# An expert layer that gathers rows of expert_v (and, for 64 tokens, of expert_u) in place of dense products

## The chip, the core and the metric
The kernel runs on one core of a Trainium2 chip. Its engines work beside each other, each in its own order of instructions: PE (TensorE, matrix products), DVE (VectorE), ACT (ScalarE), POOL (GpSimd) and SP, which only issues transfers here. The metric is the device time of one execution in microseconds, as the median of several runs; lower is better.

## What is computed
Two blocks are applied to 256 tokens of width 2048, all in float32. The first has a token mixer and then an expert layer; the second has gated linear attention with forgetting attention, and a state space layer. The change lies in the expert layer. With h the normed and modulated tokens, it is, shortened:

```python
def peer(h, w_pq, sub_keys, expert_u, expert_v):
    q = (h @ w_pq).reshape(B, T, 8, 2, 128)                      # 8 heads, two half keys
    s = einsum('bthpd,hpnd->bthpn', q, sub_keys)                 # 128 scores for each half key
    s1, i1 = top_k(s[..., 0, :], 16);  s2, i2 = top_k(s[..., 1, :], 16)
    cand_s, cand_i = all 256 sums s1 + s2, and i1 * 128 + i2
    top_s, pos = top_k(cand_s, 16);    idx = cand_i[pos];   g = softmax(top_s)
    act = gelu(einsum('td,ted->te', h, expert_u[idx]))           # 128 experts for a token
    return einsum('te,ted->td', g * act, expert_v[idx])
x = x + g2 * peer(...)
```

expert_u and expert_v have 16,384 rows of 2048 float32 each, 128 MB a table. Each token uses 128 rows of each.

## The kernel before
**Order of the work.** The program is written as one stream of main work, and side work is written as generators that wait in lists (`bg`, `bg2`, `bg3` and so on). `pump` takes the next piece of each list; the main loops call it at a rate set by `rate[0]` (pieces for each two sub-steps). So the place of side work in every engine's order is fixed when the program is built. `flush` runs what is left. `page` gives one of the 8 KB-wide buffers that all stages share, and an instruction that writes a page waits until its last user is done.

**Split products.** PE multiplies in a fast format that keeps only the upper part of a float32. A float32 operand is therefore split in two: ACT copies it into the fast format (`whi`, line 117) and DVE subtracts that copy from it (`wlo`, line 118). A product is then three matmuls: high by high, high by low, low by high.

**Dense expert layer.** After the key projection (`h2_part` makes the high and low parts `h2h` and `h2l` of the tokens, 16 slices of 128 channels), `u_unit(n)`, n from 0 to 63, computes the activation of all 16,384 experts for all 256 tokens. One unit takes two blocks of 128 experts: two loads of 1 MB of `u_t` (expert_u laid out by channels) from SP, the split, and 96 matmuls of 128x256 (lines 1281, 1282, 1286). ACT applies gelu, and POOL stores the unit's activations to `scr_a` in memory (line 1289).

Beside the units, `choose` finds for each token the 128 experts and the gates. `scatter(half, G)` turns these into a dense matrix of gates for one half of the experts: DVE makes one-hot matrices, POOL multiplies them by three parts of the gate (line 1362 before the change), PE multiplies the pair in bf16 (line 1377) and ACT copies the result out.

`Half.run` is the second product. For each block of 128 experts of its half, 1 MB of expert_v is loaded in rows from SP, split, and multiplied by the gated activations, in four banks of 512 columns for two tiles of 128 tokens (lines 1419, 1420, 1422). The order is: 47 units, with the first `scatter`; half 0 (`v0.run`), with `s5_prep`, which makes power tables for the state space layer; the other units, with the second `scatter`; half 1 (`v1.run`), whose last banks are finished one by one by `x2_end` and turned by `x2_turn` for the next projection.

**What follows.** The projection `ab_w_in` of the second block (lines 180 to 189) runs with `s5_prep2` as side work, which makes the other tables of the state space layer: DVE products, and 256 small matmuls (line 542).

In the names of tiles, `mm` and `sm` are PSUM banks, `raw` is a loaded block of weights, `x1T` holds the tokens by channels.

## Time and profile before

| | us |
|---|---|
| median of 3 runs | 3764.72 (3762.97 to 3765.24) |
| the profiled execution, its own time | 3766.24 |
| its span, first to last instruction | 3764.5 |
| PE busy | 3589.0 (95%) |
| DVE busy | 2660.7 (71%) |
| ACT busy | 1786.7 (47%) |
| POOL busy | 786.9 (21%) |

The mean granted clock of PE is 0.985 of its full speed. The program moves 754.19 MB, 200 GB/s in the mean. Busy time is no bound by itself: the stages have different limits, so the table is to be read together with windows of the trace, one for each stage, and with the times at which a stage begins and ends.

### The profile page before, as it was taken

The page shows a single profiled execution, that of the slowest core. Times are in us where ns is not written, and L with a number is a line of the kernel's source. Part 1 is how long each engine was busy: PE and PEld are TensorE (multiplying, and loading weights), DVE is VectorE, ACT ScalarE, POOL GpSimd, SP SyncE. Part 2 cuts the span into 40 slices and gives each one's busy share as a digit, 9 for nine tenths or more (in the row PEclk, how much of TensorE's full clock was granted, in tenths as well). Part 3 has the DMA queues.
Part 4 walks back from the last instruction along what each step waited for, and adds up shares of the span by engine and source line. Part 5 has one row for each costly group of instructions (what it writes and reads, how often), then busy time and mean ns, then how long its engine had stood idle before and what let it go on. Part 6 is the DMA issues. An engine that isn't in the chain of part 4 may idle for free.

```text
span 3764.5 us, 64975 instructions
## 1 busy us (share of the span) xinstructions
PE 3589.0 (95%) x24610; PEld 3151.5 (84%) x24610; DVE 2660.7 (71%) x4569; ACT 1786.7 (47%) x3619; POOL 786.9 (21%) x779
## 2 busy tenths in 40 slices
PE   6999999999999999999999998999999999988998
PEld 3788878887779999999887888888879977887896
DVE  2456896777658588887887589866577666677765
ACT  4323535644455444555545455555454445523464
POOL 2202210100101013554020067200042022142200
PEclk8999999999999999999999999999999999999999
DMA  9554573377654555555667544666545535675454
GB/s 370 223 224 166 173 254 122 108 273 269 239 186 155 198 191 194 196 186 197 243 235 261 190 141 155 253 224 218 197 160 201 190 111 185 222 210 182 147 198 166
DMA packets 155242, 754.19 MB, mean 200 GB/s; under 512 B 40608, under 2 KB 40896, under 8 KB 76464
## 3 DMA queue, kind: packets, MB, share of 16 engines
q1 hardware_dynamic: 116224, 661.78, 49.9%
q0 software_dynamic: 29232, 84.07, 6.9%
q10 hardware_dynamic: 9472, 4.20, 0.4%
q8 instruction: 192, 3.15, 0.3%
q14 instruction: 122, 1.00, 0.1%
HBM read 716.65 MB, written 33.19 MB: 199 GB/s over the span
## 4 chain that ended last, share of the span: by engine, by line
PE 77%; DVE 9%; DMA 5%; issue 4%; POOL 3%; ACT 2%; DVEq 0%; ACTq 0%; POOLq 0%; SPq 0%
PE mm L189 15%; PE mm L180 7%; PE mm L183 7%; PE mm L181 7%; PE sm L1281 5%; PE sm L1282 5%; PE sm L1286 5%; PE mm L1422 3%; PE sm L1422 3%; PE mm L1419 3%; PE sm L1420 3%; PE mm L1420 3%; PE sm L1419 3%; DVE wlo L118 3%; POOL oh L1362 1%
## 5 line engine op out<-in xcount | busy, mean ns | idle before, releaser
L118 DVE TENSOR_TENSOR wlo<-raw,whi 128x512 fp32r<-128x512 f32 x2096 | 1567.3, 765 | 844.1 <-ACT whi L117 749.9
L117 ACT CAST whi<-raw 128x512 fp32r<-128x512 f32 x2096 | 1274.5, 621 | 1607.9 <-PE mm L181 319.8
L1281 PE MATMUL sm<-h2h,whi 128*128 128x256 f32 x2048 | 513.6, 284 | 1.0 <-ACT whi L117 1.0
L1282 PE MATMUL sm<-h2l,whi 128*128 128x256 f32 x2048 | 507.4, 281 | 0.0
L1281 PEld LDWEIGHTS sm<-h2h,whi 128*128 128x128 f32 x2048 | 388.4, 190 | 1.2 <-ACT whi L117 1.2
L1282 PEld LDWEIGHTS sm<-h2l,whi 128*128 128x128 f32 x2048 | 387.4, 189 | 0.0
L1286 PE MATMUL sm<-h2h,wlo 128*128 128x256 f32 x2048 | 326.7, 281 | 10.3 <-DVE wlo L118 10.3
L1362 POOL TENSOR_TENSOR oh<-e,gpart 128x512 bf16<-128x512 bf16 x192 | 282.0, 1493 | 134.9 <-DMA raw<-in_expert_v_dram 51.0
L1286 PEld LDWEIGHTS sm<-h2h,wlo 128*128 128x128 f32 x2048 | 278.4, 189 | 12.0 <-DVE wlo L118 11.5
L180 PE MATMUL mm<-whi,hTh 128*128 128x512 f32 x576 | 230.6, 401 | 1.3 <-ACT whi L117 1.0
L181 PE MATMUL mm<-whi,hTl 128*128 128x512 f32 x576 | 227.2, 394 | 0.0
L189 PE MATMUL mm<-hTh,whi 128*128 128x256 f32 x704 | 180.2, 291 | 5.4 <-ACT hTh L611 2.4
L189 PE MATMUL mm<-hTl,whi 128*128 128x256 f32 x704 | 177.5, 285 | 3.4 <-DVE hTl L613 3.4
L183 PE MATMUL mm<-wlo,hTh 128*128 128x512 f32 x576 | 172.7, 397 | 1.9 <-DVE wlo L118 1.7
L189 PEld LDWEIGHTS mm<-hTh,whi 128*128 128x128 f32 x704 | 133.4, 190 | 19.2 <-issue 8.3
L189 PEld LDWEIGHTS mm<-hTl,whi 128*128 128x128 f32 x704 | 134.1, 191 | 7.6 <-DVE hTl L613 4.8
L189 PE MATMUL mm<-cnh,whi 128*128 128x256 f32 x512 | 136.3, 298 | 2.9 <-ACT whi L117 2.9
L180 PEld LDWEIGHTS mm<-whi,hTh 128*128 128x128 f32 x576 | 108.7, 189 | 31.3 <-issue 3.4
L183 PEld LDWEIGHTS mm<-wlo,hTh 128*128 128x128 f32 x576 | 108.1, 189 | 29.0 <-DVE wlo L118 3.8
L189 PE MATMUL mm<-cnl,whi 128*128 128x256 f32 x512 | 130.2, 287 | 0.0
L181 PEld LDWEIGHTS mm<-whi,hTl 128*128 128x128 f32 x576 | 108.6, 189 | 23.4
L1289 POOL DMA_DIRECT2D scr_a<-ua x64 | 36.4, 569 | 428.8 <-ACT ua L1288 417.4
(1562 smaller groups left out, 7829.0 us busy)
## 6 DMA issues: line engine op xcount, KB each, us to landing
raw<-in_u_t_dram SPq DMA_DIRECT2D x128, 1024.0 KB, 4.9
raw<-in_expert_v_dram SPq DMA_DIRECT2D x124, 1024.0 KB, 4.8
raw<-in_w_in_dram SPq DMA_DIRECT2D x80, 1024.0 KB, 4.9
raw<-in_ab_w_in_dram SPq DMA_DIRECT2D x56, 1024.0 KB, 4.9
raw<-in_wmodA_dram SPq DMA_DIRECT2D x32, 1024.0 KB, 8.7
mraw<-in_wmodB_dram SPq DMA_DIRECT2D x32, 1024.0 KB, 8.9
raw<-in_c_w_in_dram SPq DMA_DIRECT2D x32, 1024.0 KB, 5.1
mrn<-in_wmodB_dram POOLq DMA_DIRECT2D x64, 256.0 KB, 4.2
```

Of the source, the lines that this page charges most:

```text
L117: nc.scalar.copy(out=hi, in_=src)
L118: last_split[0] = nc.vector.tensor_tensor(out=lo, in0=src, in1=hi.bitcast(F32), op=OP.subtract)
L180: nc.tensor.matmul(o, lhsT=xh, rhs=wh, start=(k == 0), stop=False)
L181: nc.tensor.matmul(o, lhsT=xl, rhs=wh, start=False, stop=False)
L183: nc.tensor.matmul(ps[i][:], lhsT=X(k, tt)[0], rhs=wl, start=False, stop=(k == K - 1))
L189: nc.tensor.matmul(o, lhsT=w[:, j * 128:(j + 1) * 128], rhs=x, start=start, stop=stop, skip_group_check=True)
L1281: nc.tensor.matmul(o, lhsT=uh, rhs=xh, start=(k == 0 and r == 0), stop=False, skip_group_check=True)
L1282: nc.tensor.matmul(o, lhsT=uh, rhs=xl, start=False, stop=False, skip_group_check=True)
L1286: nc.tensor.matmul(o, lhsT=w_, rhs=x_, start=False, stop=(k_ == 15 and r == 1), skip_group_check=True)
L1362: nc.gpsimd.tensor_tensor(out=oh1[i][:], in0=e1[:], in1=gpart[:, i, tb:tb + 8, None].to_broadcast([128, 8, 64]), op=OP.mult)
L1419: nc.tensor.matmul(self.ps[tt][b][:], lhsT=hl[tt][0], rhs=vh, start=first, stop=False)
L1420: nc.tensor.matmul(self.ps[tt][b][:], lhsT=hl[tt][1], rhs=vh, start=False, stop=False)
```

## The change
Expert_v is no longer multiplied densely. For each token, its 128 rows are gathered with an indirect DMA (128 rows of 8 KB, 1 MB, one row in each partition), and summed over partitions with the gated activations as weights. `rows_of(t)` gathers for two tokens that lie 32 apart; `add_rows` makes the sums with eight matmuls of 32x512 in float32, of which four lie side by side in the array; the weights stand in one column of a `strip` that is zero elsewhere, so that 32 steps fill 32 rows of a bank. `part` multiplies a finished bank by g2 and adds it to the tokens.

The 256 tokens are treated in two ways. For the first NS = 64, expert_u is gathered by rows, too: `near()` gathers 64 times 128 rows (two tokens, half of their experts each), DVE multiplies them by the token and sums, and after gelu the 32 steps on expert_v follow. All that is side work under the u units. For the other ND = 192 tokens, the u units still compute all experts densely, but with 32 unsplit float32 matmuls of 128x192 in a unit; ACT's queue stores the activations to `scr_a`. Then `rest()` runs 96 steps for these tokens: gather the rows of two tokens, pick their 2 x 128 activations out of `scr_a` with two more indirect DMAs of single floats (`pick`), form the weights, add the rows. Gathers run three steps ahead, picks four.

`scatter`, its one-hot matrices and the split of expert_u and expert_v go. `choose` is kept and gives expert numbers and places in `scr_a`. `s5_prep` and `s5_prep2` are both side work of `rest` now; what POOL did in them is done by DVE, and their transfers go from SP. In `h2_part` POOL adds the shift for all 16 slices, and ACT copies the sum, so that `x1T` holds the tokens in float32 for the unsplit product.

The diff, cut to its core:

```diff
 def s5_prep():
-        V, G = nc.vector, nc.gpsimd
+        V, G = nc.vector, nc.sync
...
-                    tt(w0, Rim[:, ps_, 0:m], pi, OP.mult, G)
+                    tt(w0, Rim[:, ps_, 0:m], pi, OP.mult)
...
     def h2_part(kk):
...
-        nc.scalar.activation(out=h_, in_=t, func=AF.Identity, bias=s2c[:, kk:kk + 1])
-        if kk % 3 < 2:
-            nc.vector.scalar_tensor_tensor(out=l_, in0=t, scalar=s2c[:, kk:kk + 1], in1=h_.bitcast(F32),
-                                           op0=OP.add, op1=OP.subtract)
-        else:
-            nc.gpsimd.tensor_scalar(out=t, in0=t, scalar1=s2c[:, kk:kk + 1], scalar2=None, op0=OP.add)
-            nc.gpsimd.tensor_tensor(out=l_, in0=t, in1=h_.bitcast(F32), op=OP.subtract)
+        nc.gpsimd.tensor_scalar(out=t, in0=t, scalar1=s2c[:, kk:kk + 1], scalar2=None, op0=OP.add)
+        nc.scalar.copy(out=h_, in_=t)
+        (nc.gpsimd if kk % 3 == 2 else nc.vector).tensor_tensor(out=l_, in0=t, in1=h_.bitcast(F32), op=OP.subtract)
...
-    scr_a = dr.tile([64, 128, 512], F32, name="scr_a")
-    def u_unit(n):
-        a = t2([128, 512], F32, "ua")
-        ps = smb()
-        late = []
-        for r in range(2):
-            for k, uh, ul in wstream(A["u_t"][2 * n + r], 16, 128, 16):
-                o = ps[:, r * 256:r * 256 + 256]
-                xh, xl = h2h[k // 8][:, k % 8, :], h2l[k // 8][:, k % 8, :]
-                nc.tensor.matmul(o, lhsT=uh, rhs=xh, start=(k == 0 and r == 0), stop=False, skip_group_check=True)
-                nc.tensor.matmul(o, lhsT=uh, rhs=xl, start=False, stop=False, skip_group_check=True)
-                late.append((k, ul, xh))
-                if k % 4 == 3:
-                    for k_, w_, x_ in late:
-                        nc.tensor.matmul(o, lhsT=w_, rhs=x_, start=False, stop=(k_ == 15 and r == 1), skip_group_check=True)
-                    late.clear()
-        nc.scalar.activation(out=a[:], in_=ps[:], func=AF.Gelu)
-        nc.gpsimd.dma_start(out=scr_a[n], in_=a[:])
+    NS = 64
+    ND = 256 - NS
+    scr_a = dr.tile([128, 128, ND], F32, name="scr_a")
+    def u_unit(n):
+        a = t2([128, 2, ND], F32, "ua")
+        ps = mmb()
+        for r in range(2):
+            raw = page("uraw", [128, 16, 128]) if r else stm.tile([128, 16, 128], F32, name="raw", tag="raw", bufs=2)
+            nc.sync.dma_start(out=raw[:], in_=A["u_t"][2 * n + r])
+            for k in range(16):
+                if k % 4 == 0:
+                    half_step[0] += rate[0] / 2
+                    pump(int(half_step[0]))
+                    half_step[0] -= int(half_step[0])
+                nc.tensor.matmul(ps[:, r * ND:r * ND + ND], lhsT=raw[:, k, :], rhs=x1T[k // 8][:, k % 8, NS:256],
+                                 start=(k == 0 and r == 0), stop=(k == 15 and r == 1), skip_group_check=True)
+        nc.scalar.activation(out=a[:], in_=ps[:, 0:2 * ND].rearrange("p (a b) -> p a b", a=2), func=AF.Gelu)
+        nc.scalar.dma_start(out=scr_a[2 * n:2 * n + 2].rearrange("r p t -> p r t"), in_=a[:])
...
-    def scatter(half, G):
...
-    class Half:
...
+    def gather(dst, src, idx):
+        nc.gpsimd.indirect_dma_start(out=dst, out_offset=None, in_=src,
+                                     in_offset=bass.IndirectOffsetOnAxis(ap=idx.bitcast(U32), axis=0))
...
+    def rows_of(t):
+        r_ = [page("vrow", [128, 2048]) for _ in range(2)]
+        for c in range(2):
+            gather(r_[c][:], A["expert_v"], slot_e[:, t + 32 * c:t + 32 * c + 1])
+        return r_
+    def add_rows(bank, i, strip, r_, ms=(0, 1)):
+        for m in ms:
+            for g in range(4):
+                c, b = g % 2, 2 * m + g // 2
+                nc.tensor.matmul(bank[m][g * 32:g * 32 + 32, :], lhsT=strip[:, c, 31 - i:63 - i],
+                                 rhs=r_[c][:, b * 512:b * 512 + 512], start=(i == 0), stop=(i == 31),
+                                 tile_position=(0, g * 32), skip_group_check=True)
...
+    def near():
+        h2d = page("h2d", [128, 2048])
+        a2r, s2r = mod_row(4, "a2r"), mod_row(3, "s2r")
+        nc.scalar.activation(out=h2d[0:64, :], in_=x1[0][0:NS, :], func=AF.Copy, scale=r2[0:NS, 0:1])
+        nc.gpsimd.tensor_tensor(out=h2d[0:64, :], in0=h2d[0:64, :], in1=a2r[0:64, :], op=OP.mult)
+        nc.gpsimd.tensor_tensor(out=h2d[0:64, :], in0=h2d[0:64, :], in1=s2r[0:64, :], op=OP.add)
+        nc.gpsimd.dma_start(out=h2d[64:128, :], in_=h2d[0:64, :])
+        nc.vector.tensor_tensor(out=pair, in0=ident[:, 0:64], in1=ident[:, 64:128], op=OP.add)
+        while not chosen:
+            yield
+        rows = []
+        def load(j):
+            rows.append(page("urow", [128, 2048]))
+            gather(rows[-1][:], A["expert_u"], near_e[:, j:j + 1])
+        for j in range(3):
+            load(j)
+        yield
+        yield
+        for j in range(64):
+            t = rows.pop(0)
+            for p in range(2):
+                cs = slice(p * 1024, p * 1024 + 1024)
+                nc.vector.tensor_tensor_reduce(out=t[:, cs], in0=t[:, cs], in1=h2d[:, cs], scale=1.0, scalar=0.0,
+                                               op0=OP.mult, op1=OP.add, accum_out=near_f[:, p, j:j + 1])
+            if j < 61:
+                load(j + 3)
+            yield
+        nc.vector.tensor_tensor(out=near_f[:, 0], in0=near_f[:, 0], in1=near_f[:, 1], op=OP.add)
+        wide = t2([128, 128], F32, "wide")
+        nc.vector.memset(wide[:], 0.0)
+        for i in range(2):
+            h_ = slice(i * 64, i * 64 + 64)
+            nc.scalar.activation(out=wide[h_, h_], in_=near_f[h_, 0], func=AF.Gelu)
+        nxt = rows_of(0)
+        ps = smb()
+        nc.tensor.matmul(ps[:, 0:64], lhsT=wide[:], rhs=pair, start=True, stop=True)
+        nc.vector.tensor_tensor(out=act, in0=ps[:, 0:64], in1=slot_g[:, 0:NS], op=OP.mult)
+        near_bank.extend(smb() for _ in range(2))
+        yield
+        yield
+        for i in range(32):
+            strip = strips[i % 3]
+            nc.vector.tensor_copy(out=strip[:, :, 31], in_=act[:, i:i + 33:32])
+            add_rows(near_bank, i, strip, nxt)
+            if i < 31:
+                nxt = rows_of(i + 1)
+            yield
+            yield
+    def rest(done):
+        places = scr_a[:].rearrange("a b (c o) -> (a b c) o", o=1)
+        todo = [NS + 64 * q + i for q in range(3) for i in range(32)]
+        def pick(k):
+            a = t2([128, 2], F32, "picked")
+            for c in range(2):
+                t = todo[k] + 32 * c - NS
+                gather(a[:, c:c + 1], places, slot_a[:, t:t + 1])
+            return a
+        rows = {k: rows_of(todo[k]) for k in range(3)}
+        acts = {k: pick(k) for k in range(4)}
+        last = []
+        for k, t in enumerate(todo):
+            i, q = k % 32, k // 32
+            if k == 1:
+                g2.append(mod_row(5, "g2"))
+            if k == 3:
+                for b in range(4):
+                    part(near_bank, 0, 0, b, nc.vector)
+            if i == 0:
+                bank = [mmb() for _ in range(2)]
+            pump(4)
+            if k + 3 < len(todo):
+                rows[k + 3] = rows_of(todo[k + 3])
+            if k + 4 < len(todo):
+                acts[k + 4] = pick(k + 4)
+            strip = strips[k % 3]
+            nc.vector.tensor_tensor(out=strip[:, :, 31], in0=acts.pop(k)[:], in1=slot_g[:, t:t + 33:32], op=OP.mult)
+            if k + 2 >= len(todo):
+                last.append((i, strip, rows.pop(k)))
+                continue
+            add_rows(bank, i, strip, rows.pop(k))
+            if i == 31:
+                for b in range(4):
+                    part(bank, (q + 1) // 2, (q + 1) % 2, b, nc.vector)
+                    if q == 0:
+                        done(0, b)
+        for m in range(2):
+            for l in last:
+                add_rows(bank, *l, ms=(m,))
+            for b in (2 * m, 2 * m + 1):
+                part(bank, 1, 1, b, nc.vector)
+                done(1, b)
-    bg2.append(choose())
-    bg.append(scatter(0, G0))
-    rate[0] = 0.36
-    for n in range(UFIRST - 1):
-        u_unit(n)
...
+    bg2 += [choose(0), choose(1)]
+    bg3.append(near())
+    rate[0] = 2
+    for n in range(64):
+        u_unit(n)
+        rate[0] = 0.55
+    flush()
+    bg += [s5_prep(), s5_prep2()]
...
-    v1.run(x2_end, x2_turn)
+    rest(x2_end)
...
-    bg.append(s5_prep2())
-    rate[0] = 1.1
+    rate[0] = 0
```

How the instructions stand on the engines, at three places. First PE, in a u unit. Before, beside the first `scatter` (`oh` are one-hot matrices):

```order
L1281 MATMUL sm<-h2h_10307,whi 128x256
L1282 MATMUL sm<-h2l_10309,whi 128x256
L1286 MATMUL sm<-h2h_10307,wlo 128x256 x4
L1377 LDWEIGHTS oh_14843
L1377 MATMUL sm<-oh_14847,oh_14843 128x64
```

And after, in the units that have the 64 tokens' sums beside them (`uraw` is the unit's second block, `vrow` the gathered rows):

```order
L1382 MATMUL sm<-vrow,strip 32x512 x8
L1283 MATMUL mm<-x1T_9501,raw 128x192 x8
L1283 MATMUL mm<-x1T_9502,raw 128x192 x8
L1283 MATMUL mm<-x1T_9501,uraw 128x192 x8
L1283 MATMUL mm<-x1T_9502,uraw 128x192 x4
L1382 MATMUL sm<-vrow,strip 32x512 x8
```

The three split matmuls have become one unsplit matmul, and the eight narrow matmuls of a step (line 1382) stand where the one-hot products stood. The first 38 units have none of these; 29 of the 32 steps stand in the others.

Second POOL. Before, between the last of `s5_prep` in half 0 and the second `scatter` (line 1362 is the product of one-hot and gate there):

```order
L318 TENSOR_TENSOR s5w<-Rre,s5par 128x512
L414 DMA scr_r<-Rre 128x2x1024
L414 DMA scr_r<-Rim 128x2x1024
L441 DMA scr_p<-s5pw 128x640
L443 DMA scr_p<-s5par 128x64 x2
L1362 TENSOR_TENSOR oh_22976<-e_22974,gpart 128x512
L1362 TENSOR_TENSOR oh_22977<-e_22974,gpart 128x512
```

And after, from the middle of the u phase into `rest` (line 1362 is the indirect DMA of `gather` here):

```order
L1362 DMA urow<-in_expert_u_dram,near_e 128x2048 x54
L1362 DMA vrow<-in_expert_v_dram,slot_e 128x2048 x70
L1362 DMA picked<-scr_a,slot_a 128x1 x8
L1362 DMA vrow<-in_expert_v_dram,slot_e 128x2048 x2
L1362 DMA picked<-scr_a,slot_a 128x1 x2
L731 DMA g_15199<-scr_m_1407 128x2048
L1362 DMA vrow<-in_expert_v_dram,slot_e 128x2048 x2
```

POOL has no products left there: its row is gathers alone, 54 of expert_u, then 70 of expert_v (64 for the near tokens and 6 for the first three steps of `rest`), then two of rows and two of activations for each step. Each gather waits for the eighth software DMA before it.

Third PE, where the state space tables are made. Before, in the projection after the expert layer:

```order
L181 MATMUL mm<-whi,abl_29452 128x512
L180 MATMUL mm<-whi,abh_29450 128x512
L181 MATMUL mm<-whi,abl_29452 128x512
L183 MATMUL mm<-wlo,abh_29450 128x512 x2
L213 MATMUL sm<-ident,r_r 128x128 x2
L542 MATMUL sm<-s5c,s5bd 32x64 x8
L189 MATMUL mm<-abh_29449,whi 128x256
```

And after, in `rest`:

```order
L1382 MATMUL sm<-vrow,strip 32x512 x24
L1382 MATMUL mm<-vrow,strip 32x512 x112
L207 MATMUL sm<-ident,s5z 64x128 x8
L1382 MATMUL mm<-vrow,strip 32x512 x16
L542 MATMUL sm<-s5c,s5bd 32x64 x8
L1382 MATMUL mm<-vrow,strip 32x512
L542 MATMUL sm<-s5c,s5bd 32x64 x8
L1382 MATMUL mm<-vrow,strip 32x512 x7
```

The small matmuls of line 542 have moved from among the split matmuls of the projection to among the sums of gathered rows.

## Rows read from the trace of the kernel before

**Rows 1.** The page's shares: engine, busy us (share of the span), instructions.
```profile
PE 3589.0 (95%) x24610; PEld 3151.5 (84%) x24610; DVE 2660.7 (71%) x4569; ACT 1786.7 (47%) x3619; POOL 786.9 (21%) x779
```

**Rows 2.** Windows, expert layer: us, busy per engine, PEclk, DMA share, GB/s.
```profile
1231.00:1805.00 574.00, 565.76 (x5305) 562.59 (x5303) 448.05 (x696) 295.09 (x693) 199.42 (x152) 0.99 0.56 195
1805.00:2147.00 342.00, 338.99 (x1530) 280.59 (x1529) 263.95 (x530) 172.75 (x290) 40.63 (x43) 1.00 0.66 235
2147.00:2386.00 239.00, 220.34 (x2311) 213.15 (x2310) 203.40 (x188) 120.24 (x408) 142.97 (x105) 1.00 0.45 159
2386.00:2756.00 370.00, 361.89 (x1636) 300.10 (x1635) 240.52 (x349) 186.98 (x315) 20.74 (x17) 0.99 0.62 219
2756.00:2960.00 204.00, 195.24 (x1528) 178.43 (x1527) 158.04 (x385) 98.10 (x185) 57.51 (x55) 0.99 0.56 188
```

**Rows 3.** Timeline of PE at both ends: start us, us, engine, line, operation.
```profile
1231.13 0.36 PE L1281 MATMUL sm<-h2h,whi 128*128 128x256 f32 x1
2756.13 0.40 PE L180 MATMUL mm<-whi,abh 128*128 128x512 f32 x1
```

**Rows 4.** Timeline of POOL: two stores of activations, one for each u unit.
```profile
1290.49 0.54 POOL L1289 DMA_DIRECT2D scr_a<-ua  x1 [10.78 <-ACT ua L1288]
1301.81 0.54 POOL L1289 DMA_DIRECT2D scr_a<-ua  x1 [10.78 <-ACT ua L1288]
```

**Rows 5.** Timeline of PE: float32 matmuls of 256 and 129 columns, and one ahead.
```profile
633.76 0.64 PE L189 MATMUL mm<-hTh,wlo 128*128 128x256 f32 x4
634.24 1.89 PE L1053 MATMUL sm<-qT,kT 128*128 128x256 f32 x8
669.55 3.39 PE L1073 MATMUL sm<-vm,P 128*128 128x129 f32 x28 [0.98 <-DVE P L1064]
```

**Rows 6.** Groups of DVE by form: instruction, count | busy, mean ns | idle.
```profile
L682 DVE SCALAR_TENSOR_TENSOR macc<-mraw,sil,macc 128x2048 f32<-128x2048 f32 x30 | 70.4, 2345 | 2.1 <-DMA mraw<-in_wmodB_dram 2.1
```

**Rows 7.** Timeline of PE in the first stage: four narrow matmuls side by side.
```profile
53.86 1.94 PE L578 MATMUL sm<-raw,silz 128*32 128x512 f32 x8
100.09 1.06 PE L578 MATMUL sm<-raw,silz 128*32 128x512 f32 x8
101.09 0.62 PE L189 MATMUL mm<-hTh,wlo 128*128 128x256 f32 x3
```

**Rows 8.** Windows in the first stage, columns as in rows 2.
```profile
20.00:60.00 40.00, 25.05 (x134) 13.83 (x132) 9.93 (x32) 19.08 (x44) 2.56 (x4) 0.74 1.01 421
55.00:60.00 5.00, 4.30 (x29) 2.30 (x25) 0.94 (x6) 3.02 (x6) 0.64 (x2) 0.88 1.01 398
```

**Rows 9.** The page's DMA queues: packets, MB, share of 16 engines over the span.
```profile
q1 hardware_dynamic: 116224, 661.78, 49.9%
q10 hardware_dynamic: 9472, 4.20, 0.4%
```

**Rows 10.** DMA issues: engine, count, KB each, median us from issue to landing.
```profile
raw<-in_u_t_dram SPq DMA_DIRECT2D x128, 1024.0 KB, 4.9
scr_a<-ua POOLq DMA_DIRECT2D x64, 256.0 KB, 3.1
raw<-in_w_in_dram POOLq DMA_DIRECT2D x8, 1024.0 KB, 9.0
```

**Rows 11.** Groups of POOL by form, columns as in rows 6.
```profile
L1289 POOL DMA_DIRECT2D scr_a<-ua x64 | 36.4, 569 | 428.8 <-ACT ua L1288 417.4 <-DVE wlo L118 11.3
L1809 POOL DMA_DIRECT2D Tm<-scr_k x16 | 21.2, 1333 | 6.7 <-DVE vt L1797 5.5 <-PE sm L1913 1.2
L1362 POOL TENSOR_TENSOR oh<-e,gpart 128x512 bf16<-128x512 bf16 x192 | 282.0, 1493 | 134.9 <-DMA raw<-in_expert_v_dram 51.0 <-DVE e L1358 35.9 <-PE sm L1282 18.5
```

**Rows 12.** Groups of PE by form, line 542, columns as in rows 6.
```profile
L542 PE MATMUL sm<-s5c,s5bd 128*32 128x64 f32 x256 | 17.3, 220 | 0.0
```

**Rows 13.** Groups of POOL by form: the shift and the low part.
```profile
L1217 POOL TENSOR_SCALAR x1T<-x1T,s2c 128x256 f32<-128x256 f32 x5 | 8.0, 1608 | 99.9 <-ACT h2h L1212 99.9
L1218 POOL TENSOR_TENSOR h2l<-x1T,h2h 128x256 fp32r<-128x256 f32 x5 | 4.5, 897 | 0.4
```

286 lines of the change are left out of this document (94 added, 192 removed).

## The prediction

> **What bounds the kernel now.** I read the shares first: TensorE is busy 3589.0 of 3764.5 us [rows 1], so nearly every stage is its own. Then I cut the expert layer into stretches [rows 2]. It runs from the first matmul on expert_u, at 1231.13, to the first matmul of the next projection, at 2756.13 [rows 3]: 1525.0 us, in which PE is idle for 574 - 565.76 = 8 us, 3, 19 and 8 us in the four stretches, 38 us in all. Meanwhile the core moves only 159 to 235 GB/s. So this layer is bound by the number of columns that PE streams, and memory has room. In an undisturbed stretch one u unit (two blocks of 128 experts) takes 1301.81 - 1290.49 = 11.32 us [rows 4], which is 96 matmuls of 0.118 us. In the first 574 us 47 units are done, 12.2 us each, since the gate scatter shares PE.
>
> The change trades PE work for memory work, so the reader should price each of the two new phases twice, once by PE and once by bytes, and take the larger.
>
> **u phase: unsplit float32 for 192 tokens, all 64 units.** A unit has now 32 matmuls of 128x192. A float32 matmul shows as two records in the trace. Eight records of 256 columns take from 634.40 (633.76 + 0.64, the end before) to 636.13, 0.216 us each; 28 records of 129 columns end 3.39 us after their start, or (3.39 - 0.16)/28 = 0.115 us each, where 0.16 is the pipeline's fill (0.28 shown for a matmul that is spaced 0.12) [rows 5]. Between them 192 columns give 0.165 us by a straight line, 0.162 in proportion to columns. A unit has 64 records: 10.4 to 10.6 us. That is only 7% less than 11.32: the column count falls from 96 x 256 = 24,576 to 64 x 192 = 12,288, but a float32 record takes twice as long for a column. Sixty-four units: 664 to 700 us (the upper end allows 0.171 for a load of weights that isn't hidden); I take 680. ACT and DVE no longer split u, so they can't be late here.
>
> **64 near tokens, under the u phase.** u by rows is 64 gathers of 1 MB and 128 multiply-and-sum instructions of 128x1024 on DVE. The nearest row is a DVE instruction on 128x2048 float32 at 2345 ns [rows 6], so a gather's pair should cost 2.3 us, with 2 to 5 us as bounds, against some 30 units x 10.6 / 64 = 5.0 us that a gather has: hidden. v by rows is 32 steps of 8 narrow matmuls of 32x512, four side by side in the array. The same form runs in the first stage: 8 records (4 matmuls) take 1.0 us (100.09 to 101.09), and 1.94 at half clock [rows 7]. A step is 2.0 us; the order puts 29 steps into the u phase: +58. The one-hots go, POOL's 282.0 us [rows 11] and the matmuls that they feed; what PE lost to them lies inside the 1525.
>
> Now bytes. In the first stage the engines are full for 40 us and move 421 GB/s, 398 in the slowest 5 us [rows 8]; at 421 a transfer of 1024 KB (1 MB here, 1.049e6 bytes) takes 2.49 us. In units 7 to 37 lie 64 gathers, 61 loads of u and 6 MB of stored activations: 131 x 2.49 = 326 us beside 30 x 10.55 = 317 of PE. In the rest of the phase it is 70 gathers, 54 loads and 5 MB, 321 us beside 26 x 10.55 + 58 = 332. So both stand nearly level, and I add 10 us of stalls (0 to 40). u phase: 680 + 58 + 10 = **748** (722 to 798).
>
> **rest: v by rows for 192 tokens.** 96 steps of two 1 MB gathers, 6 of the 192 already issued: 186 x 2.49 = 463 us. Each step has also two gathers of 128 single floats. No row has packets of 4 bytes. The nearest are the 9472 small ones of q10, 4.20 MB in 0.4% of 16 engines' span [rows 9]: 0.004 x 16 x 3764.5 us / 9472 = 25 ns each. 256 packets over 16 engines would be 0.4 us a step, 38 us in all; 0 and 80 are my bounds, 40 my value. The state space tables, g2 and final_w add some 12 MB, 30 us. Two transitions (the first picks wait for the last stored activations, which take 3.1 us to land [rows 10], and the two last steps are held for the end) 15. rest: **548** (500 to 610). PE needs 2.0 to 4 us for a step of 5.7, so it is idle half the time and no bound even at half clock. DVE has the tables' work, which before cost at most all its 263.95 and 158.04 busy us of two stretches that were full of other work [rows 2]; it fits in 548.
>
> After rest come the last sums and the turn into the next projection, before hidden under banks of matmuls: +10 (5 to 15).
>
> **POOL's queue.** Every gather is issued from POOL, four to a step, and the order shows them in a row on POOL: vrow x2, picked x2. A direct DMA costs POOL 569 ns, one in 512 pieces 1333 [rows 11]. Four issues are 2.3 to 5.3 us a step against 5.7 for the bytes: just hidden, and if not it decides (second rival). Each issue also waits for the eighth DMA before it on that queue, which keeps four row gathers in flight: 4 x 2.49 us, and direct loads of that size land in 4.9 us [rows 10].
>
> **Tables moved.** s5_prep2 leaves the stage of the next projection. There it had 256 matmuls on line 542, 17.3 us [rows 12], and part of PE's 204 - 195.24 = 8.8 idle us [rows 2]. I take -15 (bounds -10 and -26). Its DMAs now go on SP, on which nothing waits in rest; the matmuls stand among the gathers' sums, where PE has room.
>
> **h2_part.** POOL now adds the shift for all 16 slices ahead of ACT's copy, 16 x 1.61 + 5 x 0.90 = 30.2 us [rows 13], where the first block of the key projection has 16 x 12 x 0.118 = 22.7 us of PE: +6 (0 to 12).
>
> **Sum**, against the profiled execution: 748 + 548 + 10 - 1525 = -219; -15 + 6: -228. 3766.2 - 228 = 3538. That execution lies 1.5 us over the median of the runs, so **3537** is the forecast.
>
> **Rivals.**
> *1. The gathers don't reach the stream's rate.* The bytes of the two phases are 281e6 and 209e6 (stored activations and tables with them). The direct loads of the whole run, q1, moved 661.78 MB in 49.9% of 16 engines' span [rows 9], 661.78e6 / (0.499 x 3764.5 us) = 352 GB/s while they ran. At that rate the phases take 798 and 594 us; with 10 and 55 of stalls and picks 808 + 649 + 10 = 1467, and 3766.2 - 58 - 9 = 3699. For it: no row shows a row gather, and 1 MB on POOL's queue took 9.0 us to land where SP's took 4.9 [rows 10]. Against it: q1 has small packets too (5.7 KB in the mean), a gathered row is 8 KB, as in the direct load of expert_v, and 40 us at 421 are no peak of a moment. Level with before at 490e6 / (1525 + 9 - 75 us) = 336 GB/s.
>
> The Trainium skill, "DMA: Bandwidth & Descriptors", Specifications, gives about 358 GB/s as a core's limit from HBM; by that figure the sum would be an estimated 3676. The 421 of [rows 8] stand above it, so the trace doesn't agree, and the sum goes by the rows.
>
> *2. Slower: POOL's issue is the bound.* In rest POOL works through 380 issues one after another. If an indirect one costs T, rest is 380 x T as soon as that is over 548, from T = 1.44 us. Level with before at rest = 548 + 228 = 776, T = 2.04. At 2.5 us rest is 950 and the time 3940. For it: issue time on POOL grows with pieces, 569 ns to 1333 [rows 11], and an indirect DMA has 128 addresses to read. Against it: 512 pieces cost but 1.33, and 64 issues stand at 569 ns beside a DVE that was busy 448 of 574 us [rows 2]. The Trainium skill, "SBUF — State Buffer", the "DVE blocks DMA" trap, says that some DVE modes lock POOL out while it writes descriptors; these 569 ns don't show that.
>
> *3. The u phase waits.* PE and memory are level there; if the pages that gathers, h2d and u share come free late, each of 64 units may lose 1 to 3 us: 3600 to 3730.
>
> *4. Nothing in it.* If unsplit float32 were no faster than 11.32 a unit and both phases ran as rival 1, little were left: 64 x 11.3 + 58 + 10 + 649 + 10 = 1450, and with rival 3's waits on top 3730 to 3790.
>
> **Chances.** Forecast, 3465 to 3610: 0.60. Rivals 1 and 3, 3610 to 3740: 0.18. Rival 4: 0.04, half of it within 0.2% of before. Rival 2 and what else ends slower: 0.15. Below 3465: 0.03. The range 3465 to 3740 holds 0.78, close to eight in ten. 0.2% (7.5 us) is about what a measurement of this kernel can tell from no change: faster by more 0.82, within 0.02, slower 0.16.
>
> **What would show it.** Right: a u unit of 10.4 to 10.6 us in units 0 to 6, 12.5 after unit 38; the share of DMA near 1.0 and 390 to 425 GB/s from unit 7 to the end of rest; a step of rest 5.3 to 6.2 us; POOL waiting for DMAs, not issuing; the next projection's 204 us shortened by 10 to 26. Wrong: windows of rest at 300 GB/s with POOL's issues back to back (rival 2), or with POOL waiting and DMA share under 0.9 (rival 1); PE waiting for u loads (rival 3); float32 records of 192 columns over 0.175 us.

## The result, and the profile after

| | us |
|---|---|
| forecast | 3537 (3465 to 3740) |
| after, median of 4 runs | 3659.99 (3658.43 to 3669.56) |
| before, median of 4 runs beside them | 3763.84 (3758.38 to 3765.24) |
| ratio, 95% interval | 0.9733 (0.9721 to 0.9745) |
| profiled execution of after: own time, span | 3658.43, 3656.7 |

The kernel became 104 us faster. The sign and the range held; the size was less than half of the 227 forecast.

The two ends of the expert layer, and of its phases, stand in PE's timeline (start us, us, engine, line, operation; in brackets the idle time before, and what ended it):

```profile
2038.38 5.36 PE L1382 MATMUL sm<-vrow,strip 128*32 128x512 f32 x48
2053.52 6.90 PE L1382 MATMUL mm<-vrow,strip 128*32 128x512 f32 x48 [9.78 <-issue]
...
2660.56 1.92 PE L1382 MATMUL mm<-vrow,strip 128*32 128x512 f32 x12 [0.45 <-DMA vrow<-in_expert_v_dram,slot_e]
...
2664.33 0.73 PE L180 MATMUL mm<-whi,abh 128*128 128x512 f32 x2 [0.24 <-ACT abh L248]
```

The first unit starts at 1239.56 (1231.13 in [rows 3]). The u phase ends with the last narrow sums of `near`, at 2038.38 + 5.36 = 2043.7; `rest` ends at 2662.5; the next projection begins at 2664.33. Against the forecast's terms:

| term | forecast | measured |
|---|---|---|
| before the first unit (`h2_part`) | +6 | +8.4 |
| u phase | 748 | 804 |
| of it 64 units | 680 | 64 x 10.40 = 666 |
| of it 29 steps of sums | 58 | 29 x 2.07 = 60 |
| what is left: stalls, and the last 3 steps of sums | 10 | 78 |
| `rest` | 548 | 619 |
| from there to the next projection | 10 | 2 |
| behind it, 3656.7 - 2664.3 against 3764.5 - 2756.1 | -15 | -16 |

The miss of 120 us is thus 56 in the u phase and 63 in `rest` and its tail; everything else came out within 3 us. Of the 78, PE is idle for 54. Another 5.4 are the last three steps of sums (line 1 above), which the forecast's sum left out. Windows of PE alone in the u phase (us, busy, mean granted clock, DMA share, GB/s) show where:

```profile
1400.00:1500.00 100.00, 87.95 (x514) 0.95 1.02 424
1500.00:1600.00 100.00, 75.76 (x429) 0.88 1.00 414
1600.00:1700.00 100.00, 90.25 (x548) 0.95 0.77 281
1700.00:1800.00 100.00, 100.00 (x644) 1.00 0.91 347
1800.00:1900.00 100.00, 100.00 (x648) 1.00 0.96 368
```

From 1400 to 1600 the DMA engines are full, and PE is idle for 36 of 200 us; from 1600 the engines have room again. From 1700 to 2000 PE never stops. What PE waits for in the whole phase is u:

```profile
PE mm L1283 <- DMA raw<-in_u_t_dram: 49.3, 9, 13.5
```

And the windows of `rest`:

```profile
2040.00:2100.00 60.00, 26.27 (x132) 0.72 0.71 276
2100.00:2200.00 100.00, 48.50 (x280) 0.78 0.75 291
2200.00:2300.00 100.00, 65.96 (x412) 0.88 0.94 354
2300.00:2450.00 150.00, 108.69 (x414) 0.90 0.97 372
2450.00:2600.00 150.00, 109.21 (x415) 0.91 0.97 366
```

The forecast took 421 GB/s from [rows 8]. The first 230 us of `rest`, where the state space tables stand, run far under it, and the settled part, which is only rows, picks and sums, still 12% under. The operations that no row of before showed are now in the groups (line, engine, operation, count | busy us, mean ns | idle before):

```profile
L1362 POOL DMA_INDIRECT vrow<-in_expert_v_dram,slot_e x256 | 252.8, 988 | 502.5 <-PE mm L1283 175.0
L1420 DVE CUSTOM_DVE_ANT_0 urow<-urow,h2d 128x1024 f32<-128x1024 f32 x128 | 156.2, 1255 | 115.0 <-DMA urow<-in_expert_u_dram,near_e 85.0
L1362 POOL DMA_INDIRECT picked<-scr_a,slot_a x192 | 186.8, 973 | 108.3 <-issue 58.8
```

An indirect issue costs POOL 0.97 to 0.99 us in the mean, whether it brings 1 MB or 512 bytes, inside the 0.57 to 1.33 of [rows 11]; back to back they stand 1.25 us apart. Four of them are 5.0 us a step. The second rival, which decides from 1.44, is out. The DVE pair takes 2.5 us (2.3 forecast) and is hidden.

### The profile page after: what moved, and what is told of

It reads as the page before. It is cut to its first block, busy times and chain, and to the rows that moved or that the text cites. A ratio compares the mean times of both kernels' runs of the same rounds, so it can differ in the third digit from the quotient of the medians.

```text
span 3656.7 us, 51912 instructions
## 1 busy us (share of the span) xinstructions
PE 3237.9 (89%) x20002; PEld 2593.6 (71%) x20002; DVE 1845.5 (50%) x3741; ACT 1062.0 (29%) x2012; POOL 899.5 (25%) x959
## 5 line engine op out<-in xcount | busy, mean ns | idle before, releaser
L118 DVE TENSOR_TENSOR wlo<-raw,whi 128x512 fp32r<-128x512 f32 x1088 | 766.2, 720 | 539.1 <-ACT whi L117 458.1
L117 ACT CAST whi<-raw 128x512 fp32r<-128x512 f32 x1088 | 660.1, 620 | 941.7 <-PE mm L181 347.6
L1382 PE MATMUL mm<-vrow,strip 128*32 128x512 f32 x1536 | 383.2, 695 | 184.1 <-issue 90.5
L1283 PE MATMUL mm<-x1T,raw 128*128 128x192 f32 x2048 | 358.9, 334 | 49.3 <-DMA raw<-in_u_t_dram 49.3
L1283 PEld LDWEIGHTS mm<-x1T,raw 128*128 128x128 f32 x2048 | 345.5, 196 | 60.9 <-issue 60.9
L1362 POOL DMA_INDIRECT vrow<-in_expert_v_dram,slot_e x256 | 252.8, 988 | 502.5 <-PE mm L1283 175.0
L1283 PE MATMUL mm<-x1T,uraw 128*128 128x192 f32 x2048 | 350.3, 328 | 0.6 <-DMA uraw<-in_u_t_dram 0.6
L1283 PEld LDWEIGHTS mm<-x1T,uraw 128*128 128x128 f32 x2048 | 336.2, 191 | 16.0 <-issue 13.4
L1420 DVE CUSTOM_DVE_ANT_0 urow<-urow,h2d 128x1024 f32<-128x1024 f32 x128 | 156.2, 1255 | 115.0 <-DMA urow<-in_expert_u_dram,near_e 85.0
L1362 POOL DMA_INDIRECT picked<-scr_a,slot_a x192 | 186.8, 973 | 108.3 <-issue 58.8
```

Of the source, the lines that this page charges most:

```text
L117: nc.scalar.copy(out=hi, in_=src)
L118: last_split[0] = nc.vector.tensor_tensor(out=lo, in0=src, in1=hi.bitcast(F32), op=OP.subtract)
L1283: nc.tensor.matmul(ps[:, r * ND:r * ND + ND], lhsT=raw[:, k, :], rhs=x1T[k // 8][:, k % 8, NS:256], start=(k == 0 and r == 0), stop=(k == ...
L1362: nc.gpsimd.indirect_dma_start(out=dst, out_offset=None, in_=src, in_offset=bass.IndirectOffsetOnAxis(ap=idx.bitcast(U32), axis=0))
L1382: nc.tensor.matmul(bank[m][g * 32:g * 32 + 32, :], lhsT=strip[:, c, 31 - i:63 - i], rhs=r_[c][:, b * 512:b * 512 + 512], start=(i == 0), s ...
L1420: nc.vector.tensor_tensor_reduce(out=t[:, cs], in0=t[:, cs], in1=h2d[:, cs], scale=1.0, scalar=0.0, op0=OP.mult, op1=OP.add, accum_out=nea ...
```

## The experiments: rest

All kernels but the last two were run once; the four runs of the changed kernel lie up to 11 us apart.

**Rows without picks; rows in order; two queues.** Why is `rest` slower than the stream? The first three kernels each take away one thing: the picks, the scatter of the rows over memory (blocks of expert_v that lie together, from POOL), and the single queue (one of two rows by a direct load from SP).

```diff
 def pick(k):
-    gather(a[:, c:c + 1], places, slot_a[:, t:t + 1])   # twice
+    return near_f[:, 2, 0:2]              # e1: constant activations
 def rows_of(t):                           # e2: blocks, from POOL
-    gather(r_[c][:], A["expert_v"], slot_e[:, ...])
+    nc.gpsimd.dma_start(out=r_[c][:], in_=A["expert_v"][b0:b0 + 128, :])
+    # e3: for c == 1 alone, from nc.sync
```

> Leaves out the 192 gathers of single activations in rest: the weights are made from a constant in their place. In the changed kernel a settled step of rest (two row gathers) takes 5.71 us, 370 GB/s, where 421 GB/s would give 4.98. Theory A (POOL's feed): a gather holds POOL for 1.25 us (0.95 and 0.30 behind it), so four a step are 5.0 us, and with the waits for lanes and pages no queue of rows stands ready for the DMA engines. With two gathers a step POOL needs 2.5 us; the step falls to 5.0 to 5.1 us and the total by about 60 us, to 3600. Theory B (rows scattered over the table are slower to read): step stays at 5.6 to 5.7, total within 12 us of 3660. Theory C (one queue alone can't keep the engines full: the first packet of a transfer is exposed unless another queue has packets): the step stays at 5.4 to 5.7. In all three the 10 us at the start of rest, where the first picks wait for the last stored activations, go.

> In rest the two row gathers of a step become direct DMAs of the same 1 MB from POOL's queue (128 rows that lie side by side, the wrong experts); the picks stay. Theory A: POOL's issue of a step falls from 5.0 to 2.5 + 2 x 0.6 to 0.9 = 3.7 to 4.3 us, so part of the loss goes: step 5.0 to 5.4. Theory B: step 5.0, since the rows lie side by side. Theory C: step stays at 5.5 to 5.8, since it is one queue still. So C is told from the others here, and B from A in the run without picks.

> In rest one of the two row gathers of a step becomes a direct load of 1 MB from SP's queue (the wrong experts); the other gather and the picks stay. Theory C: with two queues the engines stay full, step 5.0 us, 421 GB/s, total about 3600. Theory A: POOL has three issues a step, 3.75 us, step 5.0 to 5.2. Theory B: half of the rows are scattered, step about 5.3, total about 3625.

Measured: 3583.71, 3606.48 and 3607.19 us. The same window of the three, in that order:

```profile
2300.00:2450.00 150.00, 114.38 (x485) 1.00 1.01 423
```
```profile
2300.00:2450.00 150.00, 111.84 (x467) 0.99 1.02 412
```
```profile
2300.00:2450.00 150.00, 76.40 (x438) 0.72 1.00 403
```

Scattered rows of 8 KB, without picks, move 423 GB/s: as much as the stream of [rows 8], and more than rows that lie together did with picks (412). So the rows aren't slow to read, and one queue suffices: theories B and C fall, and rival 1's reason with them. Theory A, POOL's feed, fits, but e14 below moves 408 with all four issues, so the number of issues alone doesn't make 372. All three kernels lose in the first 230 us nonetheless: from 2045 to 2272 they move 339, 319 and 334 GB/s, against 298 in the changed kernel. e3 also shows that the clock doesn't bound the steps there: 0.72 granted, and 403 GB/s.

**Picks further ahead.** Their results stand in one long buffer, so that `rest` asks for them earlier and earlier.

```diff
-    if k + 4 < len(todo):
-        acts[k + 4] = pick(k + 4)
+    while len(acts) < min(len(todo), k + 5 + k // 6):
+        acts[len(acts)] = pick(len(acts))
```

> Whole computation. The picks of activations run further ahead: four steps at the start of rest, one more for each six steps, up to nineteen, and land in one buffer. The same number of gathers. Theory A in its strict form (POOL's 5.0 us a step and the bytes' 5.0 us both bind, and a step waits for its picks, which land behind the rows that were issued before them): with a lead POOL issues back to back, settled steps of 5.0 to 5.2 us in place of 5.7, total 3615 to 3635. Theory A2 (it is the number of gathers alone): settled steps stay at 5.6 to 5.8, total within 12 us of 3660.

Measured: 3623.87, and 380 GB/s in the settled window, some 5.5 us a step. The time is theory A's, the step neither theory's; alone it decides nothing.

**The tables out of rest.** `s5_prep` runs beside the u units from the 38th on, with its transfers on ACT's queue, and `s5_prep2` in the next projection again, as in the kernel before.

```diff
+        if n == 38:
+            bg.append(s5_prep())
         u_unit(n)
     flush()
-    bg += [s5_prep(), s5_prep2()]
```

> Whole computation. The tables leave rest: s5_prep is side work of the u units from the 38th on, with its transfers on ACT's queue, and s5_prep2 goes back into the stage of the next projection, as in the kernel before. Theory T (the tables' instructions on DVE and PE stand in line with the strips and sums of rest, pages come free late and the engines run dry: 297 GB/s for the first 227 us, a loss of 67 us): rest falls from 619 us to 550 to 575; the projection takes back the 16 us that the change gave; total 3605 to 3630. Theory U (the start of rest is slow for another reason, such as the picks): rest stays over 600 and the total rises by 10 to 16.

Measured: 3568.88; `rest` goes from 619 to 509 us, the u phase doesn't grow, and what follows `rest` takes back 21 us (1013.8 against 992.4). That is more than theory T's 550 to 575, since the settled part is faster, too (405 GB/s from 2300 to 2450). In the first 227 us of `rest` after this edit (busy of PE, weight loads, DVE, ACT, POOL, then clock, DMA share, GB/s), and in the changed kernel:

```profile
2045.00:2272.00 227.00, 160.36 (x676) 32.46 (x676) 20.59 (x63) 7.05 (x18) 162.44 (x173) 0.94 0.94 379
```
```profile
2045.00:2272.00 227.00, 117.10 (x703) 40.30 (x706) 121.44 (x503) 6.58 (x17) 122.43 (x114) 0.77 0.79 298
```

DVE is busy for 121 of 227 us with the tables: it has time enough, as the forecast said. What is missing is another order. In the changed kernel, POOL's, PE's and DVE's timelines around 2095 to 2133:

```profile
2092.09 0.95 POOL L1362 DMA_INDIRECT picked<-scr_a,slot_a  x1 [0.30 <-issue]
2116.48 0.94 POOL L1362 DMA_INDIRECT vrow<-in_expert_v_dram,slot_e  x1 [23.44 <-DVE Rre L394]
2121.22 11.83 POOL L1362 DMA_INDIRECT vrow<-in_expert_v_dram,slot_e  x1 [3.80 <-DMA scr_r<-Rre]
```
```profile
2094.44 3.29 PE L1382 MATMUL mm<-vrow,strip 128*32 128x512 f32 x16 [11.61 <-DVE Rim L395]
2116.34 7.71 PE L1382 MATMUL mm<-vrow,strip 128*32 128x512 f32 x48 [18.61 <-DVE strip L1478]
```
```profile
2115.54 0.67 DVE L318 TENSOR_TENSOR Rim<-Rim,s5w 128x512 f32<-128x512 f32 x1
2116.14 0.29 DVE L1478 TENSOR_TENSOR strip<-picked,slot_g 128x2 f32<-128x2 f32 x3
2121.31 0.69 DVE L318 TENSOR_TENSOR Rre<-Rre,s5par 128x512 f32<-128x512 f32 x1
2131.55 0.68 DVE L318 TENSOR_TENSOR Rim<-Rim,s5w 128x512 f32<-128x512 f32 x1
```

From 2095 to 2116 DVE works without a gap, on table products and, for 5.4 us, on `part` of the near tokens. Behind them stand three weight strips (the group of 3 at 2116.14). Until they are written PE can't sum; when they come, it sums three steps at once. POOL stands for 23 us before a gather, and the trace names table work as what it waits for: DVE at 2116.48, when PE has only begun to sum, and before the next gather the store of a table (`scr_r<-Rre`), whose tile lies in a shared page. The DMA engines move nothing from 2102 to 2116.5. The products fit into a step by their sum and not by their place.

The gather at 2121.22 shows a second cost. It holds POOL for 11.83 us, to 2133.05, while DVE runs 18 products of 128x512 back to back, the last until 2132.23; from 2125 to 2133 the engines move 24 GB/s. Other kernels have such issues, too (11.88 and 11.72 us in e12, 11.88 and 13.90 in e13, 11.87 in e14), and each of these ends 0.8 to 0.9 us behind the end of such a run. It isn't so every time: beside e14's second run of products, from 2104 to 2115, nine issues pass at 0.94 to 0.97 us. What decides isn't shown.

**Why the settled part stays at 372.** e5 and e12 (below) have the same picks and the same work of POOL, and move 410 and 405. Two more runs took one number each: rows four steps ahead instead of three, and five pieces of side work before each step instead of four, which changes only the first 230 us.

```diff
-        rows = {k: rows_of(todo[k]) for k in range(3)}    # e13
+        rows = {k: rows_of(todo[k]) for k in range(4)}
-            pump(4)                                        # e14
+            pump(5)
```

> The changed kernel with one edit: a step's two rows are gathered four steps ahead instead of three (the picks stay where they are). In its settled stretch (2300 to 2450) the changed kernel moves 372 GB/s, POOL waits 18.3 us there for something that the trace doesn't name, and TensorE's 414 matmul records of the rows stand up to 2 us apart with no releaser shown, where the kernel with 2 own buffers moves 405 with the same picks and the same POOL work. Theory G (a row's page comes free late because the matmuls that read it end late; the gathers behind it then leave the DMA engines dry): one step more of distance covers it, the settled stretch moves 400 to 410, steps of 5.1 us, and 90 settled steps x 0.6 us = 40 to 60 us fewer for the kernel. Theory H (the DMA engines are slower in this kernel by themselves, whatever is ahead): 365 to 380 GB/s and the time within 15 us of the changed kernel's.

> The changed kernel with one number changed: five pieces of background work, the tables among them, are taken from the list before each step of rows instead of four, so that only the first 230 us of that stretch are ordered otherwise; the settled part has the same instructions in the same order. Theory P (the settled 372 GB/s are a state that the start of the stretch leaves behind, since nothing in a step makes up what the step before lost): after another start the settled part moves 400 to 410 GB/s and the time falls by 25 to 60 us. Theory H (the order of a settled step itself gives 372): 365 to 380, and the time moves by no more than 20 us.

Measured: 3607.98 and 3607.81. Their settled windows:

```profile
2300.00:2450.00 150.00, 78.39 (x466) 0.80 1.01 405
```
```profile
2300.00:2450.00 150.00, 108.50 (x454) 1.00 1.01 408
```

The order of a settled step is the same in e14, and so are the bytes: 372 isn't what such a step costs, but a state that the start leaves behind, and one step more of distance covers it. Theory H falls; e14 meets P's figures and e13 G's. How the state keeps itself up can be seen in part. POOL and PE from 2300 to 2450 in the changed kernel, and PE in e14:

```profile
POOL vrow L1362 <- remote: 18.3, 11, 3.2
PE mm L1382 <- issue: 26.4, 34, 1.8
```
```profile
PE mm L1382 <- DMA vrow<-in_expert_v_dram,slot_e: 37.2, 54, 2.1
```

POOL makes eleven pauses for something that the trace doesn't name, and PE 34 with no releaser shown; e14 has neither, and its PE waits for rows. PE's come first: from 2345 to 2353 its records stand up to 2 us apart while POOL still issues back to back, and POOL's first pause ends at 2354.39. The clock isn't excluded as a part of it. With one queue and three steps ahead, the rate goes with the granted clock: 372 GB/s at 0.90, 380 at 0.95 (e7), 405 to 410 at 0.99 to 1.00 (e5, e12, e14). Where 403 to 411 are moved at 0.69 to 0.80, rows are four ahead or there is a second queue (e13, the last two kernels, e3). No kernel held all else and changed the clock. A step has 5.0 us of POOL's issues (4 x 1.25) and 2.097 MB / 421 GB/s = 4.98 us of bytes. With two resources at the same length there is nothing with which a lost microsecond could be made up. What each pause waits for stays open.

## The experiments: the u phase

**Gathers further apart, or fewer.** First theory: 64 gathers with three in flight crowd out the loads of u. e4 releases two gathers with each unit, through a copy of their indices on ACT behind the unit's gelu, and raises the rate of side work from 0.55 to 0.7; e5 keeps two in flight.

```diff
+        with tc.issue_after(gelu.ins):                         # e4
+            nc.scalar.copy(out=e[:], in_=near_e[:, c:c + 2])
-                load(j + 3)                                     # e5
+                load(j + 2)
```

> Whole computation. Two gathers of expert_u are let go after each u unit (their row numbers are copied by ACT behind that unit's gelu), where they ran ahead freely. Theory D (the gathers run ahead and take the DMA engines from the loads of u: 24 units then lose 71 us to late loads, and the engines idle a quarter of the time in the 90 us behind): at 2 gathers a unit 4.2 MB are 10.4 us beside 10.4 us of PE, so the units from the sixth to the thirty-eighth take 10.4 to 11.0 us and the u phase falls from 804 to 740 to 760 us; total 3600 to 3620. Theory E (the loads of u wait for pages, whatever the gathers do): u phase stays at 790 to 810.

> Whole computation. The gathers of expert_u for the near tokens run two ahead of DVE, not three; nothing else is changed. Theory D (free-running gathers take the engines from the loads of u, while the phase as a whole has bytes to spare): with two in flight the gathers take more than 24 units, and the loads of u come in time more often; the stalls of the u units fall from 71 us to 20 to 45, total 3615 to 3640. Theory E (the loads of u are late because SP waits for pages and issues them one at a time, whatever the gathers do): u phase stays within 12 us of 804.

Measured: 3675.37 and 3624.11. Both miss: e4's u phase grows to some 864 us, with the DMA engines at only 0.71 to 0.85 while PE waits, e5's to 817. (e5's time is inside theory D's range, but its gain is in `rest`, at 410 GB/s: the state above.) So it isn't the number of bytes in flight. SP's waits in the u phase of the changed kernel say what it is (us in total, times, longest):

```profile
SPq L1277 <- PE mm L1283: 421.1, 58, 24.5
SPq L1277 <- DMA urow<-in_expert_u_dram,near_e: 114.7, 15, 17.7
SPq L1277 <- PE sm L1382: 108.3, 17, 10.7
```

SP issues the loads of u in order. The second load of each unit (`uraw`) takes a page of the common pool, and the page may be one that a gathered row of expert_u, or a row of expert_v that PE hasn't summed yet, still holds. Then SP stands, and the load behind it, whose own buffer is free, stands as well. The two kinds don't alternate in SP's order, either: often two `uraw` stand ahead of the `raw` that PE needs next. One stall, in PE's and SP's timelines:

```profile
1493.59 5.36 PE L1283 MATMUL mm<-x1T,uraw 128*128 128x192 f32 x32
1512.43 7.67 PE L1283 MATMUL mm<-x1T,raw 128*128 128x192 f32 x32 [13.48 <-DMA raw<-in_u_t_dram]
```
```profile
1485.72 11.93 SPq L1277 DMA_DIRECT2D uraw<-in_u_t_dram  x2
1497.76 0.37 SPq L1277 DMA_DIRECT2D raw<-in_u_t_dram  x1
```

PE needs `raw` at 1498.95; SP has issued it at 1497.76. The group of two `uraw` ahead of it was issued at 1485.72 and 1497.32, and between them SP stood, for 8.4 us at a gathered row that was still landing. The stall costs more than its 13.5 us: the 32 records behind it take 7.67 us, at a mean granted clock of 0.70, where 32 took 5.36 ahead of it, at 1.00.

**Two own buffers.** The second load of a unit gets two pages of its own, used in turn. That is the whole edit, but with it SP's order changes, too: `raw` and `uraw` now alternate, one every 5.2 us.

```diff
+    own_u = [page("uraw", [128, 16, 128]) for _ in range(2)]
-            raw = page("uraw", [128, 16, 128]) if r else ...
+            raw = own_u[n % 2] if r else ...
```

> Whole computation. The changed kernel with one edit: the second load of each u unit goes to one of two buffers of its own. The tables stay in rest, the gathers of expert_u run free. Theory E (the u units lose 71 us because SP's loads stand behind shared pages that gathered rows hold): u phase falls from 804 us to 735 to 755, total 3595 to 3620. Theory D (the engines are full of gathered rows, and the loads share what is left): u phase stays over 785.

Measured: 3554.26. SP's list of waits for its loads of u has one line left, and the window in which PE lost most is full:

```profile
SPq L1279 <- PE mm L1285: 675.4, 124, 17.0
```
```profile
1500.00:1600.00 100.00, 100.00 (x618) 1.00 1.02 423
```

The u phase ends at 1989.4, 752 us after its first unit began (1237.1), against 748 of the forecast. Units take 10.40, 12.45 with a step of sums and 14.5 with two, but for two (24.1 and 17.7: the transposes of `choose`, and a wait for ACT). From 1400 to 1600 both kernels issue 39 gathers, and their engines are equally full; but the changed kernel issues 32 loads of u in that time, and this one 38. The bytes fit, as forecast; they came in the wrong order. What the free pages did and what the alternating order did isn't told apart. Of the 106 us that the edit is worth, 52 are the u phase and 47 `rest`, which falls into the 405 state here. The 47 needn't be the buffers' own: e14 gains as much without them.

**Together.** e10 is e6 with the own buffers; e9 is e10 with e4's pacing and its rate of 0.7.

> Whole computation; the run with the tables out of rest is the base (3569). Added: the second load of each u unit goes to one of two buffers of its own, in turn, where it took whichever shared page came next; SP's order then alternates strictly between the two kinds. Theory E (a load of u stands behind a page that a gathered row still holds, or behind another load that does): the stalls of the u units fall from 70 us to under 35, total 3530 to 3540. Theory D (the free-running gathers fill the DMA engines, and loads of u share what is left): stalls stay at 55 to 80, total 3555 to 3575.

> Whole computation; the same two buffers, and the gathers of expert_u are let go two at a time behind each u unit's gelu, as in the first paced run; the tables are out of rest. Theory D: at two gathers a unit the engines carry 4.2 MB in 10.4 us, so the units from the seventh to the fortieth take 10.4 to 10.9 us, stalls under 25 us, u phase 735 to 755 us and total 3500 to 3525. If the units still take 14 us every second time, as in the first paced run, then it is the release itself, two rows at once in front of a load of u, and neither D nor E.

Measured: 3548.92, between the two theories' times, and 3529.98, 5 us over its own. In e10 units 13 to 26 take 10.3 to 10.5 us each, and then one lump of some 50 us follows: ACT stands 59.7 us at a load of tables that waits for a page which a gather holds, and gelu stands behind it. The tables on ACT's queue took SP's place as the one that waits in order. Pacing, which made e4 worse, goes with 19 us less here.

The last two bring the findings together: own buffers, rows four ahead, `s5_prep` beside the units (from the 42nd or 44th) with its first loads on POOL's queue, `s5_prep2` back in the projection; the second with pacing.

```diff
-        V, G = nc.vector, nc.sync             # in s5_prep
+        V, G = nc.vector, nc.scalar           # and its first loads from nc.gpsimd
+        if n == 42:                           # 44 with pacing
+            bg.append(s5_prep())
```

> Whole computation, all that helped: own buffers for the u units' second loads; s5_prep beside the u units from the 42nd on (its first loads on POOL's queue, so that ACT does not wait for a page), s5_prep2 in the next projection; rows of rest four steps ahead, not three. By E the u phase is 740 to 755 us, and rest 490 to 500 with settled steps of 5.1 us; the projection gives 16 us back. 3664 - (804 - 748) - (619 - 495) + 16: total 3490 to 3515.

> Whole computation: as the kernel with all that helped, and the gathers of expert_u let go two at a time behind each u unit. Under E the release brings nothing more, as the loads of u are in time anyway: within 12 us of the unreleased kernel. Under D it is 20 to 40 us faster than that.

Measured, 4 runs each beside 7 of the kernel before (3761.28): 3522.56 (3521.34 to 3528.75), ratio 0.9369 (0.9353 to 0.9385); and **3510.70** (3505.06 to 3515.73), ratio 0.9338 (0.9322 to 0.9353). The first lies 8 us over its forecast. The second lies 12 us under the first, at the edge between its two theories; it is the fastest kernel of this case, 250 us under before. Its `rest` settles at once:

```profile
2100.00:2200.00 100.00, 54.78 (x308) 0.75 1.01 410
2200.00:2300.00 100.00, 57.18 (x304) 0.69 1.01 406
```

## Why the prediction was right in its direction and wrong in its size

- **Unit, sums, DVE pairs, `h2_part`, `s5_prep2`: right.** 10.40 us a unit, 2.07 a step of sums, 2.5 a pair, +8.4 and -16. These were read from rows of the same shape or a near one, and these rows held.
- **"Gathered rows at 421 GB/s": right as a rate.** e1 moves 423, e12 423 to 424 from 1400 to 1700 in the u phase. The Trainium skill's 358 GB/s ("DMA: Bandwidth & Descriptors", Specifications), which the prediction set aside for the rows, lies under both. Rival 1 gave 3699, not far from the result, for a reason that e1 excludes.
- **POOL's issues "just hidden": right in size**, 5.0 us against 2.3 to 5.3. But the pair of 5.0 and 5.0 was no cover: in `rest` a step has no slack in POOL or in the DMA engines. And one issue took 11.83 us beside DVE's table products. The Trainium skill's trap ("SBUF — State Buffer", "DVE blocks DMA") says that POOL can't write descriptors while DVE runs an operation in a 2-port mode. The trace agrees in that an issue stood as long as DVE's products ran, and doesn't show their mode; the prediction's 569 ns were of direct DMAs, which gave no sign of it.
- **Stalls of the u phase, 10 us (0 to 40): wrong, 78.** The step that failed is the one that set bytes beside PE for whole parts of the phase (326 beside 317, 321 beside 332) and took level for hidden. It counted the bytes and not who waits at whose page. Rival 3 named just this, pages shared by gathers and u, at 1 to 3 us a unit; measured are 1.1 (about 72 us over 64 units). e12 shows the cause of 52 of them: with own buffers, and the order that they bring, 752. That this lies so near 748 is partly luck: the 64 units took 14 us less than the 680, and some 20 us of other waits and 5.4 of the last steps are still there.
- **The tables in `rest`, 30 us of bytes: wrong.** "DVE has the time" is true, and the wrong question. The strips stand behind table products in DVE's order, tables hold pages that the gathers need, and one issue stood for 11.83 us beside a run of products. The shares of the three aren't separated. The first 227 us run at 298 GB/s; 227 x (1 - 298/421) = 66 us lost. e6, which moves the tables, gains 110 in `rest`, that loss and the settled state together; no rival had named either.
- **The picks, 40 us of bytes: half of it.** With the engines full, settled steps move 405 to 410 GB/s with picks and 423 without (e1): 0.16 to 0.22 us a step, 15 to 21 in all. Beside that the picks take 2.5 of a step's 5.0 us on POOL, which the sum had as hidden. e1 gains 76 us, of which the state is a part.
- **The settled rate: wrong**, 370 for 421. 390 us x (1 - 370/421) = 47 us; 408 is what the same steps give from another start (e14), and 390 x (1 - 370/408) = 36 us of the 47 are that state. A settled step of 5.7 us lies inside the 5.3 to 6.2 that the prediction named as its mark, and even on its mean of 548/96; that is chance, for the forecast's 5.7 held picks at 40 us, tables and transitions, and the measured one is a slower rate. The mark was too wide to catch this.

`rest` moves 342 GB/s x 619 us = 212 MB, 503 us at 421 GB/s (the forecast had 463 + 30 of rows and tables); with these 66 and 47 that is 616 of the 619 measured. The band of 3610 to 3740 had 0.18, for rivals 1 and 3. The result lies there through the waits of rival 3 and through a loss in `rest` that no rival named; rival 1's slow rows had no part in it.

## What to carry to other kernels

When two resources come out level, ask which queue issues in order and which buffer each issue waits for; a load that the critical engine needs should never wait for a page that side work holds. Side work that fits by its busy time must also fit by its place: look for the longest piece between two small instructions that something waits for, and for the issues that a long piece may hold up. And where two resources of a step have the same length, as here, a step may keep the state in which it starts; one more step of distance, or another start, was worth 52 us each (e13, e14).

## What the runs showed of the hardware that was not expected

- An indirect DMA of 128 addresses mostly holds POOL for 0.95 us, with rows of 8 KB and with single floats alike, and the next follows after 0.30. In e12's u phase some 50 gathers took 1.30 to 1.41 us.
- An indirect issue that falls into a run of DVE products of 128x512 float32 can be held until 0.8 to 0.9 us behind the run: 11.83 us in the changed kernel, 11.88 and 11.72 in e12, 11.88 and 13.90 in e13, 11.87 in e14. Beside e14's second run nine issues passed at 0.94 to 0.97, and beside products of 128x64 they stayed at 0.95.
- Rows of 8 KB scattered over a table of 128 MB come at 423 GB/s, the rate of a stream; beside a PE that is busy 100% of the time (e12, 1400 to 1500) the engines still move 424.
- A loop of equal steps settled at 372 GB/s, and after another start at 408 (e14), and stayed near it for 300 us (372 and 366; 408 and 404). Only one run of the slower kernel was profiled; its four times lie within 0.3% of each other, which speaks against a chance of that run.
